# A hybrid decoder layer on one core: PSUM sets swapped from the first gate unit on, and one more seven-product pair per output unit

## Chip, cores and metric

One core of a Trainium2 chip. The metric is the device time of one execution in microseconds (us). TensorE (PE, matmuls; PEld is its weight load), VectorE (DVE), ScalarE (ACT), GpSimd (POOL) and SyncE (SP, which issues the weight transfers) each run their own queue of instructions in a fixed order and wait for each other by semaphores.

## The reference

The input x is 256 tokens by 4096 channels, all in f32.

```python
h = rmsnorm(x, ln_g)
proj = h @ w_in                      # 4096 x 12288
p_x, p_gate, q, k, v, a_gate, s_u, s_gate = split(proj)
y_pool = pool_mixer(p_x, w_pool, pool_scale)
y_attn = stick_breaking_attention(q, k, v)          # 16 heads of 128
y_ssm  = s5_mixer(s_u, ..., w_glu, b_glu)           # 1024 x 2048 GLU
y_pool = rmsnorm(y_pool, g_pool) * silu(p_gate)     # the same for the others
y = concatenate([y_pool, y_attn, y_ssm])
out = rmsnorm(x + y @ w_out, final_g)               # 4096 x 4096
```

Stick-breaking attention needs, for each head, the scores z, a softplus of them, a suffix sum of that over the keys, an exponential, and the product with v.

## The kernel before

**Matmuls.** Each f32 matmul is made of three in a faster format: a value is split into a rounded part hi and the rest lo, and hi·hi, hi·lo and lo·hi are added up in PSUM. For the weights ScalarE writes hi (L110, through `act`) and DVE subtracts to get lo (L98, through `tt`). The activations lie split in SBUF as xhl. A step streams a weight piece of 128 x 2 x 512 (512 KB, two k-tiles) by SP (`load`, L164), splits it (`split`), and multiplies it for both halves of the tokens (`mm_tok`, L273 to L275).

**Units.** The weights are passed through in units of 512 or 1024 columns: 16 narrow ones of w_in (512), the wide units w0 and w1 (1024: v, q and k of the last head groups), four GLU units of 8 k-tiles, the wide gate units w2 and w3, and four wide output units out0 to out3. A wide unit has 16 pairs s of k-tiles, each with two pieces (h = 0 and 1).

**Seven products.** In wide units the pairs in SEVEN use a Strassen-like scheme: a 2 x 2 block product of (two token halves) x (two k-tiles) x (two column halves) with 7 instead of 8 block products, 21 instead of 24 matmuls (`mm_seven`, L239). `split_seven` makes the differences t7 of the weights (four DVE operations of 512) and splits four combinations into ring entries. The activation sums y7 come from `row_sums`. Four of the products go to a second PSUM set and are added in at the end of the unit (`join_seven`).

**PSUM sets.** The wide part has four tiles of two banks each, b0 to b3. `start_bank` picks two for the sums of a unit; the other two are its side set, which takes the attention's scores and the transposes until the unit's first seven-product pair (s = 4), and the four products from there on. The GLU units sum in b2 and b3 in turn, and attention uses b0 and b1 meanwhile. A tile is free when the step that reads it has ended: for a GLU unit the addition of the bias on DVE (`gl`, in `finish`).

**Attention.** `attention` is a generator, advanced by `pump` beside the matmuls. Each head group has two pairs of heads. For one pair: scores and mask into ps_z on PE (L688 to L692), three steps on ScalarE (al), one on DVE (al, L107), a split (ah on ScalarE, ax on DVE), the suffix sum by PE into ps_z (L706 to L708), the exponential on ScalarE (aw), and ps_av on PE (L720 to L722). The last head group runs beside the GLU units.

**Placing.** The branch outputs come back as tiles yk and yT of 4 k-tiles and are split into xhl by `place(g)`, which also makes the row sums of the seven-product pairs. Six are taken back in w3; the last ones are put there by the gates in out0. At s = 7 of out0 `start_end` closes the pool `mid`; the loads of SP wait for its last readers.

**Rings.** Tag t4 in pool `base` has three places for t7, e7, and GLU tiles; tag k4 in `mid` has six for the tiles of the branches; the ring for split weights has 4 entries, 6 in wide units outside the GLU. The Tile scheduler sets the order of PE, DVE, ScalarE and POOL; only SP is written by hand.

Of the kernel before, what the change touches and what calls it, by code (L numbers as in the profile page):

```python
# [20 lines left out]
P = 128  # L21
# [13 lines left out]
RING_OUT = 6  # L35
K4 = 6
T4 = 3
SEVEN = (4, 6, 7, 9, 11, 13)
WIDE = 2 * NU
WIDE_KINDS = ("w0", "w1", "w2", "w3")  # L40
WARM = 8
# [27 lines left out]
def body(tc, a, out, ctx):  # L69
# [61 lines left out]

    xhl = xp.tile([P, KT, 2, L], F32R, name="xhl")

    def rsqrt_mean(dst, ss, n, mean_over, tp, tag):
        m = tp.tile([P, n], F32, tag=tag, bufs=3, name="rs_m")
        t = tp.tile([P, n], F32, tag=tag, bufs=3, name="rs_t")
        ts(m, ss, 1.0 / mean_over, ALU.mult, EPS, ALU.add)
        act(t, m, AF.Ln)
        act(dst, t, AF.Exp, scale=-0.5)
        tt(t, dst, m, ALU.mult)  # L140
        stt(t, t, -0.5, dst, ALU.mult, ALU.mult)
        stt(dst, t, 1.5, dst, ALU.add, ALU.mult)
# [41 lines left out]
        return s in sevens_of(*units[ui][:2])  # L184

    def sevens_of(kind, c):
        return SEVEN[1:] if (kind, c) == ("out", 0) else SEVEN if kind == "out" or kind in WIDE_KINDS else ()

    def flat(w):
        return w.rearrange("p k n -> p (k n)")  # L190
# [61 lines left out]

    def row_sums(s, xa, xb):
        where = state["rows"]
        t = where.tile([P, 3, P], F32, tag="t", bufs=1, name="ts")
        tt(t[:, 0, :], xa[:, P:L], xb[:, P:L], ALU.add)
        tt(t[:, 1, :], t[:, 0, :], xa[:, 0:P], ALU.subtract)
        tt(t[:, 2, :], xb[:, 0:P], t[:, 1, :], ALU.subtract)
        y = where.tile([P, 3, 2, P], F32R, tag="y%d" % s, bufs=1, name="y7")
        hi_lo(y[:, :, 0, :], y[:, :, 1, :], t)  # L260
        state["s7"][s] = y
# [618 lines left out]
        state["o"] = ep.tile([P, 2, D], F32, name="o")  # L880

    def start_bank(kind, c):
        first = {"w0": 2, "w1": 0, "w2": 0, "w3": 2}.get(kind, c % 2 * 2)
        state["side"] = 2 - first
        return [wide_bank(first + t, "pm") for t in range(2)]

# [15 lines left out]
    def finish(kind, c, n, ps):  # L902
# [5 lines left out]
        elif kind == "px":  # L908
            side_q.append(pool_unit(n, scaled(ps, "px")))
        elif kind == "pg":  # L910
            side_q.append(pool_gate(n, scaled(ps, "pgz")))
        elif kind == "sg":
            z = scaled(ps, "sgz")
            sgate[n] = dp.tile([P, 2, NU], F32, name="kept_s%d" % n)

            def sgate_gen(z=z, n=n):
                sg = mp.tile([P, 2, NU], F32, tag="k4", bufs=K4, name="sgm")
                sigmoid_of(z, sg)
                yield
                tt(z, z, sg, ALU.mult)  # L920
                G.dma_start(sgate[n], z)
                yield
            side_q.append(sgate_gen())
        elif kind == "v":
            cur["v"] = scaled(ps, "vt")
        elif kind in ("q", "k"):
            if n == 2:
                side_q.append(channels_away(kind, n, scaled(ps, kind + "z")))
                return
            t = mp.tile([P, 4, L], F32, tag="k4", bufs=K4, name=kind + "t")  # L930
            side_q.append(channels(scaled(ps, kind + "z"), t, QS if kind == "q" else 1.0))
            cur[kind] = t
            if kind == "k":
                if apool is None:
                    start_att()
                side_q.append(attention(n, cur["v"], cur["q"], cur["k"]))
        elif kind == "glu":
            bias = lp.tile([P, NU], F32, tag="bias", bufs=1, name="bias")
            side_dma(bias, a["bgl"][n:n + 1, :].partition_broadcast(P))
            y = bp.tile([P, 2, NU], F32, tag="t4", bufs=T4, name="gl")  # L940
            for t in range(2):
                tt(y[:, t, :], ps[t], bias, ALU.add)
            if n % 2 == 0:
                def gate_gen(y=y):
                    sg = bp.tile([P, 2, NU], F32, tag="t4", bufs=T4, name="gs")
                    glu["sg"] = sg
                    sigmoid_of(y, sg)
                    yield
                side_q.append(gate_gen())
            else:  # L950
                def val_gen(y=y, n=n):
                    tt(y, y, glu.pop("sg"), ALU.mult)
                    yield
                    square_sums(glu_sums, y, n // 2)
                    yield
                    glu[n // 2] = y
                    if n == 3:
                        r = branch_norm(glu_sums, 1024)
                        for u in range(2):
                            yu, sg = glu.pop(u), sgs[u]  # L960
                            for t in range(2):
                                stt(sg[:, t, :], yu[:, t, :], r[:, t:t + 1], sg[:, t, :], ALU.mult, ALU.mult)
                            gates.append(transposed(sg, keep(2 + u)))
                        yield
                sgs = []
                if n == 3:
                    for u in range(2):
                        sgs.append(mp.tile([P, 2, NU], F32, tag="k4", bufs=K4, name="sgb"))
                        G.dma_start(sgs[u], sgate[u])
                side_q.append(val_gen())  # L970
        elif kind in WIDE_KINDS:
            e = state["joined"]
            parts = [(k, scaled_wide(ps, e, h, k + "z")) for h, (k, _) in enumerate(WIDE_IN[c])]
            for h, (k, z) in enumerate(parts):
                if k == "v":
                    away("v", 2 + h, z.rearrange("p t (c m) -> p (t c) m", m=L))
                elif k in ("q", "k"):
                    t = mp.tile([P, 4, L], F32, tag="u4", bufs=2, name=k + "t")
                    side_q.insert(h, channels(z, t, QS if k == "q" else 1.0))
                    cur[k] = t  # L980
                else:
                    gates.append(att_gate(2 * (c - 2) + h, z))
            if c == 0:
                side_q.append(attention(2, *fetch(2, "vqk")))
            elif c == 1:
                side_q.append(attention(3, *fetch(3, "v"), cur["q"], cur["k"]))
        elif kind == "out":
            o, e, fg = state["o_n"], state["joined"], state["fg"]
            for t in range(2):
                tt(o[:, t, :], ps[t].rearrange("p h m -> p (h m)"), o[:, t, :], ALU.add)  # L990
                act(e[t].rearrange("p h m -> p (h m)"), o[:, t, :], AF.Square, accum_out=out_sums[:, t, n:n + 1])
            for t in range(2):
                tt(o[:, t, :], o[:, t, :], fg, ALU.mult)
# [21 lines left out]
    for i, (ui, s, h) in enumerate(subs):  # L1015
# [46 lines left out]
            split(split_to)  # L1062
            split_to += 1
        if ui == LATE_AT:
            if s in SEVEN:
                load_again(s)
            if s - 1 in SEVEN:
                sums_of_x(s - 1)
        if kind == "w3" and s in (2, 4, 6, 8, 10, 12) and h == 0:
            take_back(s // 2 - 1)  # L1070
# [1 line left out]
        if seven(i):  # L1072
            if h == 0:
                if s == sevens_of(kind, c)[0]:
                    assert not state["held"]
                    pp = products()
                mm_seven(i, s, ps, pp, s == sevens_of(kind, c)[0], s == SEVEN[-1])
                if s == SEVEN[-1]:
                    if kind == "out":
                        state["fg"] = load_fg(c)  # L1080
                    state["joined"] = join_seven(pp, state["o_n"] if kind == "out" else None)
        else:
            pair = htiles.pop(i)
            late = i >= N_SUB - HELD
            into = [ps[t][:, h, :] for t in range(2)] if wide else ps
            mm_tok(into, rows, (2 * s, 2 * s + 1), pair, s == 0, s == nk // 2 - 1, (0,) if late else (0, 1))
            if late:
                delayed.append((s, h, pair))
        if s == nk // 2 - 1 and h == (1 if wide else 0):
            n = nth.get(kind, 0)  # L1090
            nth[kind] = n + 1
# [26 lines left out]
                ssm_steps[0] += 1  # L1118

    o, last, fg = state["o"], state["o_n"], state["fg"]  # L1120
    sums = cp.tile([P, 2, 2], F32, name="last_sums")
    for t in range(2):
        for h in range(2):
            cols = slice(h * NU, h * NU + NU)
# [2 lines left out]
                    if h1 == h:  # L1127
                        mm_tok([None, ps[1][:, h, :]], xhl, (2 * s, 2 * s + 1), pair, False, s == KT // 2 - 1, (1,))
            tt(last[:, t, cols], ps[t][:, h, :], last[:, t, cols], ALU.add)
            act(state["joined"][t][:, h, :], last[:, t, cols], AF.Square, accum_out=sums[:, t, h:h + 1])  # L1130
        tt(out_sums[:, t, 3:4], sums[:, t, 0:1], sums[:, t, 1:2], ALU.add)
        r = cp.tile([P, 1], F32, name="r_out%d" % t)
        ss = cp.tile([P, 1], F32, name="ss_out%d" % t)
        V.tensor_reduce(ss, out_sums[:, t, :], mybir.AxisListType.X, ALU.add)  # L1134
        rsqrt_mean(r, ss, 1, D, cp, "rs")
        rows = slice(t * P, t * P + P)
        for at, wide, eng in ((0, 512, V), (512, 512, S), (1024, 1024, V), (2048, 1024, S), (3072, 1024, V)):
            cs = slice(at, at + wide)
# [110 lines left out]
```

## Time and profile before

| | |
|---|---|
| three runs, median (lowest to highest) | 1541.36 us (1539.26 to 1542.06) |
| the profiled execution | 1541.24 us |
| its span, first to last instruction | 1539.5 us |
| mean granted clock of TensorE | 0.993 |
| PE / DVE / ScalarE busy | 98% / 82% / 58% of the span |
| matmuls | 6827 |

The span is shorter than the execution by 1.7 us, which lie around it. In a row of a view, L273 is line 273 of the kernel; `pm<-hi,xhl` reads "written <- read", by the program's names without buffer numbers. A row of waits is: engine, what it was about to do, what ended the wait; total, times, longest. In a timeline row an idle time before the instruction stands in square brackets. Matmuls are pipelined, so the distance from start to start counts and not the length of a row.

### The profile page before, as it was taken

What the parts mean: (1) busy time and instruction counts of PE and PEld (TensorE: products, weight loads), DVE (VectorE), ACT (ScalarE), POOL (GpSimd) and SP (SyncE); (2) the same over time, 40 slices, a digit from 0 to 9 for tenths busy, and PEclk for the clock granted to TensorE, in tenths of its full rate; (3) what the DMA queues carried; (4) which work ended last, traced back from release to release, by engine and by line L of the source; (5) the groups of instructions that cost most, each with busy time, mean ns of one, the idle gap of its engine ahead of it and who ended that gap; (6) DMA issues with size and microseconds to landing.
All of it is one profiled execution on the core that took longest, in us unless ns stands there. A gap on an engine that the chain in (4) does not pass through costs nothing.

```text
span 1539.5 us, 19528 instructions
## 1 busy us (share of the span) xinstructions
PE 1513.6 (98%) x6827; PEld 1234.3 (80%) x6827; DVE 1267.7 (82%) x1933; ACT 897.4 (58%) x1194; POOL 20.4 (1%) x39
## 2 busy tenths in 40 slices
PE   9999999999999999999999999999999999999996
PEld 7888888888888887888787878778888878888885
DVE  7479878898988878987778787669899988988886
ACT  7655456665555655565655555756767654645453
POOL 0000000000000000000000000000000100000000
PEclk9999999999999999999999999999999999999998
DMA  9766656576666556655656756556586595666654
GB/s 356 298 227 198 203 173 209 182 223 214 207 199 197 185 166 207 199 178 160 235 192 204 266 172 223 169 213 244 170 296 219 187 332 169 234 196 207 211 198 171
DMA packets 99315, 326.70 MB, mean 212 GB/s; under 512 B 12368, under 2 KB 18256, under 8 KB 99216
## 3 DMA queue, kind: packets, MB, share of 16 engines
q1 hardware_dynamic: 84096, 296.44, 57.6%
q0 software_dynamic: 4976, 18.09, 3.1%
q10 hardware_dynamic: 10144, 10.92, 2.3%
q8 instruction: 53, 0.87, 0.2%
q14 instruction: 46, 0.38, 0.1%
HBM read 309.68 MB, written 12.58 MB: 209 GB/s over the span
## 4 chain that ended last, share of the span: by engine, by line
PE 90%; DVE 3%; DMA 3%; ACT 1%; issue 1%; SPq 0%; DVEq 0%; ACTq 0%
PE pm L273 24%; PE pm L274 24%; PE pm L275 24%; PE p L239 7%; PE pm L239 5%; DMA w<-in_ws 3%; DVE lo L98 2%; DVE t L98 1%; PE ps_y L649 1%; ACT hi L110 1%; PE ps_c L780 1%; PE ps_bu L622 0%; PE ps_z L688 0%; PE ps_p L431 0%; PE ps_t L340 0%
## 5 line engine op out<-in xcount | busy, mean ns | idle before, releaser
L110 ACT ACTIVATE hi<-w 128x1024 fp32r<-128x1024 f32 (+1 forms) x505 | 509.7, 1017 | 411.8 <-PE pm L275 335.3
L98 DVE TENSOR_TENSOR lo<-w,hi 128x1024 fp32r<-128x1024 f32 (+1 forms) x505 | 587.7, 1172 | 165.0 <-ACT hi L110 161.8
L274 PE MATMUL pm<-lo,xhl 128*128 128x512 f32 x1672 | 656.9, 393 | 0.7 <-DVE lo L98 0.7
L275 PE MATMUL pm<-hi,xhl 128*128 128x512 f32 x1672 | 655.7, 393 | 0.0
L273 PE MATMUL pm<-hi,xhl 128*128 128x512 f32 x1672 | 647.8, 393 | 1.3 <-DVE ss_out L1134 0.8
L273 PEld LDWEIGHTS pm<-hi,xhl 128*128 128x128 f32 x1672 | 315.1, 189 | 71.4 <-issue 2.9
L274 PEld LDWEIGHTS pm<-lo,xhl 128*128 128x128 f32 x1672 | 315.4, 189 | 69.3 <-issue 2.5
L275 PEld LDWEIGHTS pm<-hi,xhl 128*128 128x128 f32 x1672 | 315.2, 188 | 68.1 <-issue 2.1
L110 ACT ACTIVATE hi<-t 128x1024 fp32r<-128x1024 f32 x94 | 99.0, 1059 | 67.3 <-DVE t L98 26.2
L98 DVE TENSOR_TENSOR lo<-t,hi 128x1024 fp32r<-128x1024 f32 x94 | 113.4, 1222 | 12.8 <-ACT hi L110 12.2
L98 DVE TENSOR_TENSOR t<-w 128x512 f32<-128x512 f32 x84 | 54.4, 689 | 33.0 <-DMA w<-in_ws 32.9
L239 PE MATMUL p<-hi,y 128*128 128x512 f32 x188 | 74.1, 394 | 2.5 <-ACT hi L110 2.5
L239 PE MATMUL pm<-hi,xhl 128*128 128x512 f32 x188 | 74.1, 395 | 0.2 <-ACT hi L110 0.2
L239 PE MATMUL p<-hi,xhl 128*128 128x512 f32 x188 | 74.0, 395 | 0.0
L98 DVE TENSOR_TENSOR t<-w,t 128x512 f32<-128x512 f32 x84 | 57.7, 687 | 0.2
L107 DVE SCALAR_TENSOR_TENSOR et<-et,pw,tr 128x16 f32<-128x16 f32 (+3 forms) x256 | 55.5, 276 | 2.0 <-ACT tr L110 1.8
L110 ACT ACTIVATE tr<-et,pw 128x32 f32<-128x32 f32 (+3 forms) x128 | 44.1, 382 | 11.1 <-DVE et L107 6.8
L239 PEld LDWEIGHTS p<-hi,y 128*128 128x128 f32 x188 | 35.4, 188 | 11.6 <-ACT hi L110 3.8
L239 PEld LDWEIGHTS pm<-hi,xhl 128*128 128x128 f32 x188 | 35.3, 188 | 8.4 <-ACT hi L110 0.7
L239 PEld LDWEIGHTS p<-hi,xhl 128*128 128x128 f32 x188 | 35.5, 189 | 8.1
L637 DVE TENSOR_TENSOR_SCAN tb<-rho,ta 128x256 f32<-128x256 f32 x64 | 40.6, 677 | 0.3
L110 ACT ACTIVATE hi<-o 128x1024 fp32r<-128x1024 f32 (+1 forms) x26 | 25.0, 976 | 26.3 <-PE pm L275 21.5
(268 smaller groups left out, 1287.3 us busy)
## 6 DMA issues: line engine op xcount, KB each, us to landing
w<-in_ws SPq DMA_DIRECT2D x501, 512.0 KB, 4.2
o<-in_ws SPq DMA_DIRECT2D x26, 512.0 KB, 4.3
xsq<-in_xr SPq DMA_DIRECT2D x8, 512.0 KB, 6.7
o<-in_xr POOLq DMA_DIRECT2D x8, 512.0 KB, 11.1
xt<-in_xT SPq DMA_DIRECT2D x15, 256.0 KB, 6.1
b<-in_bst ACTq DMA_DIRECT2D x16, 192.0 KB, 4.4
u<-uT ACTq DMA_DIRECT2D x96, 32.0 KB, 2.7
kept<-yT POOLq DMA_DIRECT2D x6, 512.0 KB, 6.0
```

Source lines behind the costliest of these rows:

```text
L98: V.tensor_tensor(o, x, y, op)
L107: V.scalar_tensor_tensor(o, x, s, y, op0, op1)
L110: return S.activation(o, x, f, **kw)
L239: T.matmul(o, stat[:, p, :], pair[q][:, n], start=start and k == 0, stop=stop and k == 2, skip_group_check=True)
L273: T.matmul(ps[t], stat[:, slot, 0, sl], hi[:, n], start=begin, stop=False, skip_group_check=True)
L274: T.matmul(ps[t], stat[:, slot, 0, sl], lo[:, n], start=False, stop=False, skip_group_check=True)
L275: T.matmul(ps[t], stat[:, slot, 1, sl], hi[:, n], start=False, stop=end, skip_group_check=True)
L637: V.tensor_tensor_scan(tb[:, c, :], rho[:, pr:pr + 1].broadcast_to([P, L]), ta[:, c, :], 0.0, ALU.mult, ALU.add)
L649: T.matmul(ps[32 * j:32 * j + 32, 0:L], cf[:, j, c, :], ss[j][:, c, :], start=c == 0, stop=c == 1, skip_group_check=True)
L780: T.transpose(ps[:, (c * 2 + t) * P:(c * 2 + t + 1) * P], z[:, t, (h * 2 + c) * P:(h * 2 + c + 1) * P], ident)
```

## The change

1. SEVEN, which the output units use, becomes (4, 6, 7, 9, 10, 12, 13): seven pairs in out1 to out3, six in out0 (without s = 4). The units w0 to w3 use SEVEN_IN = (4, 6, 7, 9, 10, 13): six as before, with 10 in the place of 11.
2. From w2 on the PSUM sets are swapped: w2 sums in b2 and b3, w3 in b0 and b1, the output units alternate from b2 and b3. As b3 is held by the last GLU unit, the first pair of w2 is staggered: token half 0 of both pieces first, token half 1 after.
3. The ts tile of `row_sums` moves from the pool `rows` into the ring t4, the GLU bias tile from the pool `late` into the ring k4.
4. At the end the sum of squares of the first column half goes into out_sums, whose reduction is done early; that of the second half is added inside the normalisation.

```diff
-SEVEN = (4, 6, 7, 9, 11, 13)
+SEVEN = (4, 6, 7, 9, 10, 12, 13)
+SEVEN_IN = (4, 6, 7, 9, 10, 13)
...
-    def rsqrt_mean(dst, ss, n, mean_over, tp, tag):
+    def rsqrt_mean(dst, ss, n, mean_over, tp, tag, plus=EPS):
...
-        ts(m, ss, 1.0 / mean_over, ALU.mult, EPS, ALU.add)
+        ts(m, ss, 1.0 / mean_over, ALU.mult, plus, ALU.add)
...
-        return SEVEN[1:] if (kind, c) == ("out", 0) else SEVEN if kind == "out" or kind in WIDE_KINDS else ()
+        if kind == "out":
+            return SEVEN if c else SEVEN[1:]
+        return SEVEN_IN if kind in WIDE_KINDS else ()
...
-        t = where.tile([P, 3, P], F32, tag="t", bufs=1, name="ts")
+        t = bp.tile([P, 3, P], F32, tag="t4", bufs=T4, name="ts")
...
-        first = {"w0": 2, "w1": 0, "w2": 0, "w3": 2}.get(kind, c % 2 * 2)
+        first = {"w0": 2, "w1": 0, "w2": 2, "w3": 0}.get(kind, 2 - c % 2 * 2)
...
-            bias = lp.tile([P, NU], F32, tag="bias", bufs=1, name="bias")
+            bias = mp.tile([P, NU], F32, tag="k4", bufs=K4, name="bias")
...
+            border = kind == "w2" and at < 2
             into = [ps[t][:, h, :] for t in range(2)] if wide else ps
-            mm_tok(into, rows, (2 * s, 2 * s + 1), pair, s == 0, s == nk // 2 - 1, (0,) if late else (0, 1))
-            if late:
+            mm_tok(into, rows, (2 * s, 2 * s + 1), pair, s == 0, s == nk // 2 - 1, (0,) if late or border else (0, 1))
+            if late or border:
                 delayed.append((s, h, pair))
+            if border and at == 1:
+                for s1, h1, pair in delayed:
+                    mm_tok([None, ps[1][:, h1, :]], rows, (2 * s1, 2 * s1 + 1), pair, s1 == 0, False, (1,))
+                delayed.clear()
...
-    sums = cp.tile([P, 2, 2], F32, name="last_sums")
+    sums = cp.tile([P, 2, 1], F32, name="last_sums")
...
-            act(state["joined"][t][:, h, :], last[:, t, cols], AF.Square, accum_out=sums[:, t, h:h + 1])
-        tt(out_sums[:, t, 3:4], sums[:, t, 0:1], sums[:, t, 1:2], ALU.add)
+            act(state["joined"][t][:, h, :], last[:, t, cols], AF.Square, accum_out=(sums if h else out_sums)[:, t, 3 * (1 - h):4 - 3 * h])
+            if h == 0:
+                ss = cp.tile([P, 1], F32, name="ss_out%d" % t)
+                V.tensor_reduce(ss, out_sums[:, t, :], mybir.AxisListType.X, ALU.add)
+                ts(ss, ss, 1.0 / D, ALU.mult, EPS, ALU.add)
...
-        ss = cp.tile([P, 1], F32, name="ss_out%d" % t)
-        V.tensor_reduce(ss, out_sums[:, t, :], mybir.AxisListType.X, ALU.add)
-        rsqrt_mean(r, ss, 1, D, cp, "rs")
+        rsqrt_mean(r, sums[:, t, 0:1], 1, D, cp, "rs", plus=ss)
```

In `load_again` and `sums_of_x` SEVEN becomes SEVEN_IN too.

The scheduler puts the instructions of the changed kernel in another order. On PE at the last GLU unit, before: pm_8874 are the sums of glu3, ps_z_8652 and ps_av_8694 the first attention pair, ps_z_8720 the second (the rows from the end of glu3 on).

```order
L275 MATMUL pm_8874<-hi_8895,hhl_8488 128x512
L706 MATMUL ps_z_8652<-ah_8664,tneg_81 128x512
L707 MATMUL ps_z_8652<-ah_8664,oneneg_82 128x2x128
...
L720 MATMUL ps_av_8694<-vt_8482,aw_8692 128x128
...
L688 MATMUL ps_z_8720<-qt_8480,kt_8481 128x256
...
L692 MATMUL ps_z_8720<-maskb_84,identb_83 128x256
L706 MATMUL ps_z_8720<-ah_8755,tneg_81 128x512
```

After, pm_8767 being glu2 (its last matmuls come first here, and the rows go on to the start of glu3):

```order
L277 MATMUL pm_8767<-lo_8802,hhl_8488 128x512
L278 MATMUL pm_8767<-hi_8801,hhl_8488 128x512
L709 MATMUL ps_z_8652<-ah_8664,tneg_81 128x512
L710 MATMUL ps_z_8652<-ah_8664,oneneg_82 128x2x128
...
L723 MATMUL ps_av_8694<-vt_8482,aw_8692 128x128
...
L691 MATMUL ps_z_8720<-qt_8480,kt_8481 128x256
...
L695 MATMUL ps_z_8720<-maskb_84,identb_83 128x256
L276 MATMUL pm_8874<-hi_8829,hhl_8488 128x512
L277 MATMUL pm_8874<-lo_8830,hhl_8488 128x512
```

The first pair's suffix sum and ps_av, which stood behind glu3, now stand ahead of it; the second pair's step from ah_8755 moved from directly behind its mask to behind 43 matmuls of glu3.

On ScalarE at the same place, before (al, ah and aw of the first pair, then al of the second; bias_8947 is the bias of glu3):

```order
L110 ACTIVATE al_8659<-ps_z_8652 128x768
L110 ACTIVATE hi_8895<-w_8845 128x1024
L110 ACTIVATE al_8659<-al_8659 128x768
L110 ACTIVATE gs_8868<-gl_8865 128x1024
L75 DMA bias_8947<-in_bgl 128x512
...
L110 ACTIVATE ah_8664<-al_8659 128x768
...
L110 ACTIVATE aw_8692<-ps_z_8652 128x768
L110 ACTIVATE al_8727<-ps_z_8720 128x768
```

After, with the biases of glu1, glu2 and glu3 (bias_8749, bias_8863, bias_8947):

```order
L111 ACTIVATE al_8659<-ps_z_8652 128x768
L111 ACTIVATE hi_8895<-w_8845 128x1024
L111 ACTIVATE al_8659<-al_8659 128x768 x2
L111 ACTIVATE ah_8664<-al_8659 128x768
L111 ACTIVATE aw_8692<-ps_z_8652 128x768
L76 DMA bias_8749<-in_bgl 128x512
L76 DMA bias_8863<-in_bgl 128x512
L76 DMA bias_8947<-in_bgl 128x512
L111 ACTIVATE al_8727<-ps_z_8720 128x768
```

The issues of three biases now stand in a row behind aw_8692, the exponential of the first pair.

On DVE in w3, before, behind lo_10091 and the first row sum (w_10047 and w_10074 are the two plain pieces of pair 10; lo_10190 to lo_10194 and t7_10185 belong to the seven-product pair 11; ts_10106 is a row sum):

```order
L98 TENSOR_TENSOR lo_10153<-w_10047,hi_10152 128x1024
L98 TENSOR_TENSOR t7_10185<-w_10136,w_10080 128x512
L98 TENSOR_TENSOR t7_10185<-w_10136 128x512
L98 TENSOR_TENSOR ts_10106<-ts_10106,yk_10104 128x128
L98 TENSOR_TENSOR yk_10104<-yk_10104 128x128
L98 TENSOR_TENSOR lo_10093<-t7_10083,hi_10092 128x1024
L98 TENSOR_TENSOR t7_10186<-w_10136,t7_10185 128x512
L98 TENSOR_TENSOR lo_10180<-w_10074,hi_10179 128x1024
L98 TENSOR_TENSOR ts_10106<-yk_10104,ts_10106 128x128
L98 TENSOR_TENSOR lo_10190<-w_10080,hi_10189 128x1024
L98 TENSOR_TENSOR lo_10192<-w_10136,hi_10191 128x512
L98 TENSOR_TENSOR lo_10194<-t7_10185,hi_10193 128x1024
```

After (lo_10161 and lo_10163 are the t7 combinations of pair 10, which is a seven-product pair now; ts_10106 and ts_10114 are the row sums of the two pairs placed there, yk_10104 the tile they come from, lo_10245 and lo_10263 pieces of later pairs):

```order
L99 TENSOR_TENSOR t7_10152<-w_10074,w_10047 128x512
L99 TENSOR_TENSOR t7_10152<-w_10074 128x512
L99 TENSOR_TENSOR ts_10114<-yk_10104,ts_10114 128x128
L99 TENSOR_TENSOR xhl_102<-yk_10104,xhl_102 128x4x256
L99 TENSOR_TENSOR y7_10110<-ts_10106,y7_10110 128x3x128
L99 TENSOR_TENSOR lo_10245<-w_10150,hi_10244 128x1024
L99 TENSOR_TENSOR lo_10161<-t7_10152,hi_10160 128x1024
L99 TENSOR_TENSOR t7_10153<-w_10074,t7_10152 128x512
L99 TENSOR_TENSOR y7_10118<-ts_10114,y7_10118 128x3x128
L99 TENSOR_TENSOR lo_10263<-w_10195,hi_10262 128x1024
L99 TENSOR_TENSOR t7_10153<-w_10047,t7_10153 128x512
L99 TENSOR_TENSOR lo_10163<-t7_10153,hi_10162 128x1024
```

The row sums of two pairs and the split of the placed tile (xhl_102) now lie between the first piece of pair 10 and its combinations lo_10161 and lo_10163.

More of the change, by code (lines that the diff above doesn't have):

```diff
@@ L1064, in body @@
         if ui == LATE_AT:
-            if s in SEVEN:
+            if s in SEVEN_IN:
                 load_again(s)
-            if s - 1 in SEVEN:
+            if s - 1 in SEVEN_IN:
                 sums_of_x(s - 1)
```

## The prediction

> **What bounds the kernel now.** The page comes first: span, busy times, the chain that ended last, one group of the matmuls.
>
> ```profile
> span 1539.5 us, 19528 instructions
> PE 1513.6 (98%) x6827; PEld 1234.3 (80%) x6827; DVE 1267.7 (82%) x1933; ACT 897.4 (58%) x1194; POOL 20.4 (1%) x39
> PE 90%; DVE 3%; DMA 3%; ACT 1%; issue 1%; SPq 0%; DVEq 0%; ACTq 0%
> ```
>
> TensorE sets the time. So a change pays by fewer matmuls or by shorter idle time of PE, and costs what it adds to that idle time. PE's waits are few; these three are the largest in the middle of the kernel:
>
> ```profile
> PE ps_z L706 <- ACT ah L110: 4.6, 1, 4.6
> PE p L239 <- ACT hi L110: 2.5, 2, 2.0
> PE ps_av L720 <- ACT aw L110: 1.9, 2, 1.0
> ```
>
> The first and the third lie at the border from the last GLU unit (glu3) to w2, the second in the first output unit (out0). The windows view shows what a wait drags behind it, and how full VectorE is. Columns: stretch, length, PE, PEld, DVE, ACT, POOL busy, granted clock, DMA share, GB/s.
>
> ```profile
> 993.50:1010.97 17.47, 10.79 (x52) 9.07 (x51) 9.89 (x13) 8.60 (x12) 0.38 (x1) 0.80 0.48 181
> 1239.00:1243.00 4.00, 4.00 (x12) 3.13 (x11) 3.49 (x5) 1.72 (x3) 0.00 (x0) 0.57 1.02 396
> 853.00:940.00 87.00, 86.33 (x384) 69.96 (x383) 69.86 (x79) 47.78 (x53) 2.66 (x5) 1.00 0.65 221
> 1094.00:1180.00 86.00, 86.00 (x382) 70.02 (x381) 81.10 (x101) 61.35 (x74) 1.08 (x2) 1.00 0.66 226
> 1180.00:1266.00 86.00, 83.97 (x365) 67.83 (x364) 75.14 (x95) 55.50 (x68) 5.85 (x9) 0.98 0.71 251
> 1142.50:1161.00 18.50, 18.50 (x81) 14.98 (x81) 18.50 (x27) 12.07 (x13) 0.00 (x0) 1.00 0.85 281
> ```
>
> Rows three to five are w1, w3 and out0. The last row is the middle of w3: PE and DVE are both busy for all of its 18.5 us. DVE has nothing to spare there; whatever is put ahead of a piece that PE needs next is paid by PE.
>
> **Fewer matmuls: -2.8 us.** A plain pair is 24 matmuls, a seven-product pair 21. Out0 goes from five such pairs to six and out1 to out3 from six to seven: 4 x 3 = 12 matmuls fewer. Their spacing is read from PE's timeline in w3, first and last of 41 steps:
>
> ```profile
> 1144.18 0.40 PE L274 MATMUL pm<-lo,xhl 128*128 128x512 f32 x1
> 1153.71 0.39 PE L239 MATMUL p<-hi,xhl 128*128 128x512 f32 x1
> ```
>
> (1153.71 - 1144.18) / 41 = 0.2324 us, times 12 is 2.8 us. (The 0.39 in the row is the length of one; they overlap.)
>
> **The tail: -0.4 us.** Between the last ScalarE sum and the normalisation stand two small DVE operations:
>
> ```profile
> 1529.10 0.16 DVE L98 TENSOR_TENSOR out_sums<-last_sums 128x1 f32<-128x1 f32 x1 [0.79 <-ACT e L110]
> 1529.30 0.16 DVE L1134 TENSOR_REDUCE ss_out<-out_sums 128x1 f32<-128x4 f32 x1
> 1529.49 0.15 DVE L104 TENSOR_SCALAR rs_m<-ss_out 128x1 f32<-128x1 f32 x1
> ```
>
> The reduction now uses the half that is ready earlier, and the addition is gone: 1529.49 - 1529.10 = 0.4 us.
>
> **The border: a stall that moves.** Rows of PE, then of ScalarE, around it:
>
> ```profile
> 981.50 0.27 PE L692 MATMUL ps_z<-maskb,identb 128*128 128x256 bf16 x1
> 993.53 0.39 PE L706 MATMUL ps_z<-ah,tneg 128*128 128x512 f32 x1
> 995.59 0.49 PE L720 MATMUL ps_av<-vt,aw 128*128 128x128 f32 x2 [0.96 <-ACT aw L110]
> 997.03 0.60 PE L688 MATMUL ps_z<-qt,kt 128*128 128x256 f32 x2
> 998.45 0.27 PE L692 MATMUL ps_z<-maskb,identb 128*128 128x256 bf16 x1
> 1003.30 0.51 PE L706 MATMUL ps_z<-ah,tneg 128*128 128x512 f32 x1 [4.58 <-ACT ah L110]
> 1010.81 0.40 PE L274 MATMUL pm<-lo,xhl 128*128 128x512 f32 x1
> ```
>
> ```profile
> 982.39 0.79 ACT L110 ACTIVATE al<-ps_z 128x768 f32<-128x768 f32 x1
> 983.08 1.05 ACT L110 ACTIVATE hi<-w 128x1024 fp32r<-128x1024 f32 x1
> 998.82 0.81 ACT L110 ACTIVATE al<-ps_z 128x768 f32<-128x768 f32 x1 [3.28 <-PE ps_z L692]
> 1005.55 0.81 ACT L110 ACTIVATE aw<-ps_z 128x768 f32<-128x768 f32 x1 [2.31 <-PE ps_z L708]
> 1006.25 1.99 ACT L110 ACTIVATE hi<-w 128x1024 fp32r<-128x1024 f32 x2
> ```
>
> Now: the attention of the last head group has two pairs. Glu3's matmuls lie between the first pair's mask (981.50) and its next step (993.53) and hide that chain. The second pair's chain is bare. From 993.53 to 1010.81 pass 17.3 us; ah and ax of two pairs (2 x 0.94), two ps_av (2 x 1.4), one ps_z (1.5) and four w2 matmuls (0.9) are about 7.1 us of them. 10.2 us are lost.
>
> After: swapping the sets and staggering w2's first pair should put work under the second chain, and by the order it does (43 matmuls of glu3 stand ahead of its ah, token 0 of w2 behind). But the bias tiles now come from the ring of six, whose free places wait for the attention output's store, and three bias issues stand on ScalarE behind the first pair's aw. Queued behind them there are the second pair's al and the weight copies. The DVE step that adds a bias frees bank 3, and glu3 writes bank 3. So PE takes the whole first pair with only five matmuls of glu2 as cover. Its path: the second pair's bare chain took 1003.30 - 998.45 = 4.85 us from mask to ah; the first pair adds 0.5 (982.39 - 981.50 instead of 998.82 - 998.45) and one weight copy, 0.95. Ah reaches PE at 981.5 + 6.3 = 987.8. From there to aw 2.25 (1005.55 - 1003.30), aw itself 0.7: bias issue at 990.75. What a bias needs:
>
> ```profile
> L98 DVE TENSOR_TENSOR gl<-pm,bias x8: 680/682/692, 955.4 to 994.3; 128x512 f32<-128x512 f32 x8
> DMA to landing us min/median/max: 3.5/4.2/5.4
> ```
>
> Landing at 994.3 to 996.2, two additions 1.3, and glu3 starts at 995.6 to 997.5, middle 996.3. Without waits it would start after the mask (0.1), five matmuls (1.2) and 3.9 of attention work, at 986.7. Lost: 8.9 to 10.8, middle 9.6, against 10.2 before; up to 1.6 more if the clock is still halved when glu3 starts. Net -1.3 to +2.2; I take 0. The Trainium skill ("SBUF — State Buffer", "The DMA setup-cost knee") gives about 2 us plus bytes over 436 GB/s for a transfer, 2.6 us for these 256 KB, an estimate from that page; by it the border would gain 1.6 more, but the trace's four landings, 3.5 to 5.4 us, are slower and decide.
>
> **W3: +4.8 us.** SEVEN_IN has 10 where 11 stood, so pairs 9 and 10 are neighbours. A seven costs DVE four 512-wide differences, one 512 and three 1024-wide subtractions, a plain pair two of 1024. Pitches, start to start:
>
> ```profile
> 1143.67 1.23 DVE L98 TENSOR_TENSOR lo<-t,hi 128x1024 fp32r<-128x1024 f32 x1
> 1144.81 0.69 DVE L98 TENSOR_TENSOR t<-w,t 128x512 f32<-128x512 f32 x1
> 1145.41 0.29 DVE L98 TENSOR_TENSOR ts<-yk 128x128 f32<-128x128 f32 x1
> 1145.61 1.23 DVE L98 TENSOR_TENSOR lo<-w,hi 128x1024 fp32r<-128x1024 f32 x1
> 1154.90 0.56 DVE L98 TENSOR_TENSOR y<-ts,y 128x384 fp32r<-128x384 f32 x1
> 1155.37 1.23 DVE L98 TENSOR_TENSOR lo<-w,hi 128x1024 fp32r<-128x1024 f32 x1
> ```
>
> 1.14, 0.60, 0.20 and 0.47 for 1024, 512, 128 and 384: a seven is 5 x 0.60 + 3 x 1.14 = 6.42 us on DVE and 21 x 0.2324 = 4.88 on PE; a plain pair 2.28 and 5.58. Two sevens in a row use up 3.1 us of DVE's lead. Up to the row at 1143.67 (lo_10091) both programs run the same order. From there the new order puts six 1024, four 512, eight 128 and one 384 up to lo_10161 (6.84 + 2.40 + 1.60 + 0.47 = 11.3): done at 1155.0. The ts tiles sit in the ring of three that the t7 pieces use, so t7_10152 and t7_10153 come late, behind two row sums. PE reaches lo_10161 37 matmuls after 1144.18, at 1152.8: it waits 2.2. The same count gives 1158.9 against 1154.4 for lo_10163 (4.6), 1160.3 against 1155.6 for lo_10200 (4.7, or 4.8 with the part by which an operation outlasts its pitch). The waits overlap; in all 4.8. Below 3.2 only if DVE brings a lead of more than 2 us to 1143.67, and above 4.8 only with a slowed clock behind it, 6.4.
>
> **Out0: -0.4 us.** Before:
>
> ```profile
> SPq L164 <- DVE xhl L98: 17.1, 3, 11.8
> 1225.86 10.40 DMA w<-in_ws
> 1238.42 0.49 PE L239 MATMUL p<-hi,y 128*128 128x512 f32 x1 [2.01 <-ACT hi L110]
> ```
>
> The SP queue stood 11.8 us until the mid tiles were free, then the loads came in a burst (a transfer of 10.4 us), a ScalarE copy waited, PE idled 2.0 us and ran 3.4 us at the 0.57 clock window above, where a matmul takes 0.43: another 3.4 x (1 - 0.23 / 0.43) = 1.6. These 3.6 us should go, since the placing steps now end a pair earlier. In their stead a sixth seven: in pairs 6 to 13 DVE needs 6 x 6.42 + 2 x 2.28 = 43.1 us against PE's 40.4; with five it was 38.9 against 41.1. The swing is 4.9, the upper end; the lower is 0. Counting the rows with the pitches leaves DVE 1.5 to 1.9 behind; with a slowed clock 3.2. Net -3.6 to +1.3; I take -0.4.
>
> **The rest: +0.3.** Neighbouring sevens in w0 to w2 and out1 to out3 find DVE less full (69.86 of 87 us in w1): 0 to 1.
>
> Sum: -2.8 - 0.4 + 0 + 4.8 - 0.4 + 0.3 = +1.5 against the profiled execution's 1541.24 us (span 1539.5 and 1.7 around it; 0.1 below the median of the runs): 1542.7, or 1542.9 beside the median. Of this kernel 0.2% (3.1 us) is about what can be told from no change.
>
> **The rivals.** *Faster: DVE keeps its lead.* If the order in w3 costs PE nothing, 4.8 go: 1538.1; if bias transfers also land before the attention ends, 3.4 more: 1534.7. For it: the scheduler had this order to choose, and out0 loses its burst. Against it: the row of 18.5 full DVE microseconds. It decides where DVE leads by 5.3 us at lo_10077 rather than by the 0.5 counted. Chance 0.24.
>
> *Slower: each new wait halves the clock.* After the 2.0 us wait PE ran 3.4 us at half pace. W3's waits (2.2, then 2.4) and glu3's late start would each do the same: +1.6, +1.6, and out0 at its upper end +1.7: 1547.8. It decides from waits of about 2 us. Chance 0.30. The Trainium skill ("TensorE: Matmul & The Clock Gate", "What's actually happening") says the clock halves after an idle window of about 3.4 us; by that w3's waits would be too short and this rival loses 1.6. The trace has a half clock after a wait of 2.0, so I let the row decide.
>
> *The stagger does nothing*, since the stall only moves to the glu2 border: that is part of the forecast. Had it fallen away whole, 10.2 less: 1532.7; the order of PE, with ah ahead of glu3, speaks against that.
>
> **How the numbers follow.** Forecast 1542.9 with a chance of 0.46 and a range of its own of 1538.5 to 1545. 0.24 lie on the faster side and 0.30 on the slower. Within 0.2% is 1538.3 to 1544.4, which holds most of the forecast's range: same 0.42, faster 0.24, slower 0.34. The range 1534 to 1548.5 leaves out a tenth on each side.
>
> **What would show it.** Right: PE waits on ah (about 4.9 us) ahead of glu3 and on a bias addition right before it, none ahead of w2; waits on lo at 1152 to 1160 in w3 that add up to 4.8; no 11.8 us of SP in out0, with some waits on lo instead. Wrong: no PE wait in w3 on DVE, or glu3 starting by 987.

## The result

The changed kernel takes 1553.31 us in the median (1552.09 to 1554.55), the kernel before beside it 1541.32 us (1539.26 to 1542.06). The ratio is 1.008, with a 95% interval of 1.0062 to 1.0097: 12 us slower, where +1.5 us were forecast and 1548.5 us was the upper end.

The page of the profiled execution (1554.55 us):

```profile
span 1552.8 us, 19543 instructions
PE 1515.8 (98%) x6815; PEld 1231.4 (79%) x6815; DVE 1283.3 (83%) x1962; ACT 902.3 (58%) x1203; POOL 20.5 (1%) x39
PE 89%; DVE 5%; ACT 3%; DMA 2%; issue 1%; DVEq 0%; ACTq 0%; SPq 0%
```

There are 12 matmuls fewer, as intended, and yet the span is 13.3 us longer; in the chain that ended last the share of DVE went from 3% to 5% and that of ScalarE from 1% to 3%. PE's largest waits, after:

```profile
PE p L242 <- ACT hi L111: 5.1, 7, 2.7
PE ps_z L709 <- ACT ah L111: 4.7, 1, 4.7
PE pm L277 <- DVE lo L99: 3.7, 4, 2.5
PE p L242 <- DVE lo L99: 2.0, 2, 1.4
PE ps_c L783 <- ACT kz L111: 1.7, 2, 1.1
PE pm L276 <- DVE gl L99: 1.2, 1, 1.2
```

The wait on ah is still there. New are the waits on lo, 5.7 us in sum, where the whole kernel before had 0.7, and the waits on hi have doubled from 2.5 us.

**Where the time went.** The table sums, stage by stage, by how much each start-to-start distance on PE exceeds the usual one (0.232 us for 512 columns, 0.118 for 256, 0.110 for 128; excesses under 0.03 left out). It so holds idle time and halved clock together. A wait ahead of the first matmul of a unit is counted with that unit. The last line is the time from PE's end to the end of the span.

| us lost | before | after | |
|---|---|---|---|
| end of the last narrow unit, and w0 | 3.0 | 9.7 | +6.7 |
| w1 | 2.0 | 3.4 | +1.4 |
| glu2 and glu3 | 10.3 | 10.4 | +0.1 |
| w2 | 1.1 | 3.4 | +2.2 |
| w3 | 0.5 | 8.0 | +7.6 |
| out0 | 4.4 | 1.8 | -2.5 |
| out3 | 1.1 | 0.0 | -1.1 |
| behind PE's end | 12.7 | 15.3 | +2.6 |

With -0.5 in the first 15 units and 12 x 0.232 = 2.8 for the matmuls this is +13.7 against +13.3 in the spans.

**The glu2 border**, PE and ScalarE after:

```profile
988.79 0.27 PE L695 MATMUL ps_z<-maskb,identb 128*128 128x256 bf16 x1
994.95 0.80 PE L709 MATMUL ps_z<-ah,tneg 128*128 128x512 f32 x1 [4.72 <-ACT ah L111]
998.06 0.79 PE L723 MATMUL ps_av<-vt,aw 128*128 128x128 f32 x2 [0.90 <-ACT aw L111]
1003.16 0.48 PE L276 MATMUL pm<-hi,hhl 128*128 128x512 f32 x1
```

```profile
997.20 0.81 ACT L111 ACTIVATE aw<-ps_z 128x768 f32<-128x768 f32 x1 [2.31 <-PE ps_z L711]
997.26 1.32 ACTq L76 DMA_DIRECT2D bias<-in_bgl  x3
```

```profile
1001.63 1.28 DVE L99 TENSOR_TENSOR gl<-pm,bias 128x512 f32<-128x512 f32 x2
```

As forecast, the stall has moved: 6.2 us from mask to ah (6.3 forecast), three bias issues at aw, glu3 14.4 us behind the mask (14.8). One sign that the prediction named is missing: PE does not wait on the bias addition ahead of glu3. The addition ended at 1002.9, and PE, which did its attention work at half clock (the granted clock was 0.62 from 989.83 to 1003.40), was done with that at 1003.1. The two paths ended 0.2 us apart. The wait on gl in the list above (1.2 us) comes 20 us later, in w2.

**W0.** PE's waits there, and SP's (the loads of weights, and by L297 those of xs, the x tiles for the row sums):

```profile
781.60 0.50 PE L277 MATMUL pm<-lo,xhl 128*128 128x512 f32 x1 [0.54 <-DVE lo L99]
787.11 0.50 PE L277 MATMUL pm<-lo,xhl 128*128 128x512 f32 x1 [2.50 <-DVE lo L99]
```

```profile
SPq L297 <- DVE ts L99: 14.5, 1, 14.5
SPq L297 <- DVE y L99: 4.1, 1, 4.1
```

The ring t4 has more users than the section on the rings lists: xs is one of them. An xs load stood 14.5 us because a ts tile held its place, and every weight load behind it on SP stood too. Before, xs waited as well, 12.2 us at the same place, but on its own predecessors:

```profile
SPq L294 <- DVE xhl L98: 16.2, 3, 12.2
```

So the length of the wait is not the loss. What changed is when SP went on, first before, then after:

```profile
752.50 0.33 SPq L294 DMA_DIRECT2D xs<-in_xT  x1
```

```profile
754.53 0.33 SPq L297 DMA_DIRECT2D xs<-in_xT  x1
```

It went on 2.0 us later, and 2.4 us later with the last xs (759.13 and 761.52). In w0 a late weight then reaches PE: DVE waits for it, and the lo that it makes after that is the one that ends PE's 2.5 us at 787.11:

```profile
784.03 1.29 DVE L99 TENSOR_TENSOR t<-w 128x512 f32<-128x512 f32 x2 [2.49 <-DMA w<-in_ws]
785.84 1.22 DVE L99 TENSOR_TENSOR lo<-w,hi 128x1024 fp32r<-128x1024 f32 x1
```

How 2.0 to 2.4 us on SP became 6.7 us on PE was not followed step by step. The half clock behind the waits is a part of it: ten matmuls from 787.11 to 791.11 took 4.0 us where 2.3 is usual.

**W3**, waits of PE in order and a window behind them:

```profile
1162.76 0.50 PE L242 MATMUL p<-hi,y 128*128 128x512 f32 x1 [0.53 <-ACT hi L111]
1164.89 0.50 PE L242 MATMUL p<-lo,y 128*128 128x512 f32 x1 [1.40 <-DVE lo L99]
1168.78 0.80 PE L242 MATMUL p<-hi,y 128*128 128x512 f32 x1 [2.70 <-ACT hi L111]
```

```profile
1165.00:1173.00 8.00, 5.30 (x14) 3.73 (x15) 6.69 (x10) 4.86 (x5) 0.00 (x0) 0.59 0.80 290
787.70:790.80 3.10, 3.10 (x9) 2.40 (x8) 2.83 (x3) 0.00 (x0) 0.00 (x0) 0.50 0.75 200
```

The first row is w3, the second w0 behind its 2.5 us wait. In w0 the granted clock was a half. In w3 it was 0.59 over 8.0 us; if it was either whole or a half there, it was a half for 8.0 x 0.41 / 0.5 = 6.6 us.

What the last and longest of the three waits in w3 waited for, on DVE and then on ScalarE:

```profile
1166.96 0.68 DVE L99 TENSOR_TENSOR t<-w,t 128x512 f32<-128x512 f32 x1
1167.67 1.06 ACT L111 ACTIVATE hi<-t 128x1024 fp32r<-128x1024 f32 x1 [3.61 <-DVE t L99]
```

From 1148.8 to 1167.6 DVE had no gap. It was late with t7, and ScalarE stood 3.6 us for it.

**The tail.** Additions of the joined products and of the sums to the output on DVE, first before, then after:

```profile
1518.50 1.23 DVE L98 TENSOR_TENSOR o<-o,e 128x1024 f32<-128x1024 f32 x1
1520.66 1.29 DVE L98 TENSOR_TENSOR o<-pm,o 128x512 f32<-128x512 f32 x2 [0.94 <-PE pm L275]
```

```profile
1532.37 1.23 DVE L99 TENSOR_TENSOR o<-o,e 128x1024 f32<-128x1024 f32 x1
1533.69 0.69 DVE L99 TENSOR_TENSOR o<-pm,o 128x512 f32<-128x512 f32 x1
1534.81 1.29 DVE L99 TENSOR_TENSOR o<-pm,o 128x512 f32<-128x512 f32 x2 [0.42 <-PE pm L278]
```

Before, the join ended 7.0 us ahead of the end of PE's last matmul (1526.77), and token half 0 could be normalised and sent while PE made half 1. After, with a seventh pair and 12 and 13 as neighbours at the end of out3, it ends 3.9 us ahead of PE's end (1537.49); half 0 is late, and half 1 waits on DVE behind it.

### The profile page after: what moved, and what is told of

Read it like the earlier page. It is cut to its first block, busy times and chain, and to the rows that moved or that the text cites. A ratio compares the mean times of both kernels' runs of the same rounds, so it can differ in the third digit from the quotient of the medians.

```text
span 1552.8 us, 19543 instructions
## 1 busy us (share of the span) xinstructions
PE 1515.8 (98%) x6815; PEld 1231.4 (79%) x6815; DVE 1283.3 (83%) x1962; ACT 902.3 (58%) x1203; POOL 20.5 (1%) x39
## 4 chain that ended last, share of the span: by engine, by line
PE 89%; DVE 5%; ACT 3%; DMA 2%; issue 1%; DVEq 0%; ACTq 0%; SPq 0%
PE pm L276 24%; PE pm L277 24%; PE pm L278 24%; PE p L242 7%; PE pm L242 6%; DVE lo L99 2%; DMA w<-in_ws 1%; ACT hi L111 1%; DVE t L99 1%; PE ps_y L652 1%; PE ps_c L783 1%; PE ps_bu L625 0%; PE ps_p L434 0%; PE ps_z L691 0%; PE ps_t L343 0%
## 5 line engine op out<-in xcount | busy, mean ns | idle before, releaser
L277 PE MATMUL pm<-lo,xhl 128*128 128x512 f32 x1640 | 643.9, 393 | 3.7 <-DVE lo L99 3.7
L278 PE MATMUL pm<-hi,xhl 128*128 128x512 f32 x1640 | 642.3, 392 | 0.0
L276 PE MATMUL pm<-hi,xhl 128*128 128x512 f32 x1640 | 635.2, 393 | 2.1 <-DVE gl L99 1.2
L277 PEld LDWEIGHTS pm<-lo,xhl 128*128 128x128 f32 x1640 | 308.9, 188 | 72.8 <-DVE lo L99 6.1
L276 PEld LDWEIGHTS pm<-hi,xhl 128*128 128x128 f32 x1640 | 308.9, 188 | 71.7 <-issue 2.9
L278 PEld LDWEIGHTS pm<-hi,xhl 128*128 128x128 f32 x1640 | 308.9, 188 | 66.5 <-issue 2.1
L111 ACT ACTIVATE hi<-t 128x1024 fp32r<-128x1024 f32 x102 | 106.9, 1058 | 103.6 <-DVE t L99 60.3
L99 DVE TENSOR_TENSOR lo<-t,hi 128x1024 fp32r<-128x1024 f32 x102 | 122.7, 1218 | 13.4 <-ACT hi L111 13.2
L242 PE MATMUL p<-hi,y 128*128 128x512 f32 x204 | 81.4, 399 | 4.9 <-ACT hi L111 4.9
L99 DVE TENSOR_TENSOR t<-w 128x512 f32<-128x512 f32 x90 | 58.0, 685 | 31.2 <-DMA w<-in_ws 31.1
L242 PE MATMUL pm<-hi,xhl 128*128 128x512 f32 x204 | 80.7, 397 | 0.3 <-ACT hi L111 0.2
L242 PE MATMUL p<-hi,xhl 128*128 128x512 f32 x204 | 79.4, 394 | 0.2 <-ACT hi L111 0.2
L242 PEld LDWEIGHTS pm<-hi,xhl 128*128 128x128 f32 x204 | 38.6, 189 | 9.5 <-ACT hi L111 1.2
L242 PE MATMUL p<-lo,y 128*128 128x512 f32 x102 | 40.8, 400 | 2.0 <-DVE lo L99 2.0
```

The costliest lines, as they stand in the source:

```text
L99: V.tensor_tensor(o, x, y, op)
L111: return S.activation(o, x, f, **kw)
L242: T.matmul(o, stat[:, p, :], pair[q][:, n], start=start and k == 0, stop=stop and k == 2, skip_group_check=True)
L276: T.matmul(ps[t], stat[:, slot, 0, sl], hi[:, n], start=begin, stop=False, skip_group_check=True)
L277: T.matmul(ps[t], stat[:, slot, 0, sl], lo[:, n], start=False, stop=False, skip_group_check=True)
L278: T.matmul(ps[t], stat[:, slot, 1, sl], hi[:, n], start=False, stop=end, skip_group_check=True)
```

## The experiments

Two theories at the start. A: the tiles that moved into shared rings (ts, bias) cost the time, the swap by itself is good. B: the denser seven-product pairs cost it. Medians of each run, with the kernel before timed on the same chip:

| run | us | before | ratio (95%) |
|---|---|---|---|
| swap_only | 1536.43 | 1541.17 | 0.9966 (0.9951 to 0.9981) |
| swap_bias | 1537.94 | 1541.17 | 0.9973 (0.9963 to 0.9983) |
| ts_only | 1546.30 | 1541.17 | 1.0029 (1.0018 to 1.0040) |
| old_sevens | 1543.41 | 1541.17 | 1.0011 (1.0001 to 1.0021) |
| ts_back | 1546.51 | 1540.87 | 1.0038 (1.0026 to 1.0051) |
| neighbours_12_13 | 1545.26 | 1540.87 | 1.0027 (1.0018 to 1.0035) |
| no_swap | 1555.09 | 1540.87 | 1.0091 (1.0077 to 1.0104) |
| swap_tail | 1535.65 | 1540.87 | 0.9963 (0.9950 to 0.9977) |
| xs_elsewhere | 1545.66 | 1541.80 | 1.0026 (1.0017 to 1.0035) |
| ts_split | 1534.02 | 1541.80 | 0.9953 (0.9939 to 0.9967) |

The time lost on PE by stage, worked out as above ("border" is glu2, glu3 and w2; w0 includes the end of the unit ahead of it):

| us lost | w0 | w1 | border | w3 | out0 | behind PE |
|---|---|---|---|---|---|---|
| before | 3.0 | 2.0 | 11.4 | 0.5 | 4.4 | 12.7 |
| after | 9.7 | 3.4 | 13.7 | 8.0 | 1.8 | 15.3 |
| swap_only | 2.8 | 2.0 | 8.4 | 0.5 | 4.5 | 12.7 |
| swap_bias | 2.7 | 2.0 | 12.5 | 0.5 | 0.5 | 12.7 |
| ts_only | 9.8 | 2.0 | 13.3 | 0.8 | 1.9 | 12.7 |
| old_sevens | 8.5 | 2.0 | 12.7 | 0.8 | 2.1 | 11.5 |
| ts_back | 3.1 | 3.4 | 12.3 | 2.4 | 8.9 | 15.4 |
| neighbours_12_13 | 6.4 | 2.0 | 12.1 | 1.7 | 4.0 | 15.3 |
| no_swap | 8.3 | 3.2 | 17.2 | 8.4 | 2.2 | 15.3 |
| swap_tail | 2.9 | 2.0 | 8.8 | 0.5 | 3.1 | 11.5 |
| xs_elsewhere | 2.1 | 3.2 | 12.6 | 8.8 | 1.9 | 15.2 |
| ts_split | 2.1 | 2.0 | 7.5 | 0.8 | 2.0 | 11.4 |

**swap_only.** The kernel before with the swap and the stagger. These lines switch them on; the other lines of the stagger are those of the change:

```diff
-        first = {"w0": 2, "w1": 0, "w2": 0, "w3": 2}.get(kind, c % 2 * 2)
+        first = {"w0": 2, "w1": 0, "w2": 2, "w3": 0}.get(kind, 2 - c % 2 * 2)
...
+            border = kind == "w2" and at < 2
```

> The kernel before with the swapped PSUM sets and w2's staggered first pair alone; the seven-product pairs, the ts tile, the bias tile and the tail stay as they were. Theory A (what cost time are the two tiles that moved into shared rings; the swap by itself is good): the order of PE puts glu3 under the first attention pair and w2 under the second, no wait on ah above 1 us, 8 to 10 us fewer at the border, 1531 to 1534 us. Theory B (the loss comes from the denser seven-product pairs, the swap has no worth): 1540 to 1543 us.

4.7 us faster, between the ranges of A and B. The wait on ah is gone from glu2 and glu3, as A has it, but not all of the 8 to 10 us came: the border as a whole gained 3.0, since w2 now loses 8.0 us, 6.8 more than before. Rows of its PE:

```profile
1026.17 0.41 PE L343 MATMUL ps_t<-ident,sgb 128*128 128x128 f32 x2 [1.69 <-issue]
1028.26 1.39 PE L343 MATMUL ps_t<-ident,sgb 128*128 128x128 f32 x8 [0.60 <-ACT yT L111]
```

The gate tiles (sgb) are transposed there, and waits on lo follow. That these steps used to be hidden in the long stall and now meet w2's matmuls is a reading that no run tested.

**swap_bias.** The same, and the bias tile in the ring:

```diff
-            bias = lp.tile([P, NU], F32, tag="bias", bufs=1, name="bias")
+            bias = mp.tile([P, NU], F32, tag="k4", bufs=K4, name="bias")
```

> The same as the run before it, and the bias tile of the GLU units in the ring k4. Theory A: the bias issues move behind the first pair's exponential, PE waits 4.5 to 5 us on ah ahead of glu3 and the gain is gone, 1540 to 1543 us, 8 to 10 above the run without it. Theory B: the bias tile is harmless, within 1.5 us of the run without it.

The stall is back at glu2 (a wait of 4.7 us on ah), the border loses 12.5 instead of 8.4. The total rose by only 1.5 us, which the intervals of the two runs do not tell from nothing, since out0 lost 0.5 instead of 4.5 in this order. So A is right on the mechanism and wrong on the total, which is where B had it.

**ts_only.** The kernel before with the ts tile in t4:

```diff
-        t = where.tile([P, 3, P], F32, tag="t", bufs=1, name="ts")
+        t = bp.tile([P, 3, P], F32, tag="t4", bufs=T4, name="ts")
```

> The kernel before with the ts tile of the row sums in the ring t4, nothing else. Theory A: the loads of xs for the row sums at the end of the last narrow unit wait for places in that ring, SP stands longer and w0 waits on lo as in the changed kernel: 4 to 7 us more, 1545 to 1548 us, nearly all of it between 755 and 800 us. Theory B: at w0 the neighbouring pairs 9 and 10 did it, and this changes nothing there, 1540 to 1543 us.

5.1 us slower; w0 loses 9.8, as in the changed kernel, with the old pairs. At w0 B has fallen.

**old_sevens.** The changed kernel with the old pairs:

```diff
-SEVEN = (4, 6, 7, 9, 10, 12, 13)
-SEVEN_IN = (4, 6, 7, 9, 10, 13)
+SEVEN = (4, 6, 7, 9, 11, 13)
+SEVEN_IN = (4, 6, 7, 9, 11, 13)
```

> The changed kernel with the old pairs (4, 6, 7, 9, 11, 13) in all wide units, so 12 more matmuls (2.8 us). Theory A: the losses of the two rings stay (6 at w0, 0.6 at the border against the kernel before), those of w3 and of the tail go: 1546 to 1550 us. Theory B: nearly all losses go, 1539 to 1543 us.

9.9 us come back, despite 12 more matmuls, and the total lies just above B's range, well below A's. W0 stays near what A says (8.5); w3 falls to 0.8, and the tail to 11.5 us, under the 12.7 of before. So each theory holds for a part: the pairs cost 7 us in w3, 3.8 in the tail and 1.4 in w1 (back at 2.0 here), the ring 5 to 7 at w0. Which of the new pairs, or their number, makes the tail late was not tried apart. From here on: C, these have nothing to do with each other; D, in w3 it takes both.

**ts_back.** The changed kernel with ts in its old place, and, for room, a constant's raw tile in k4:

```diff
-        t = bp.tile([P, 3, P], F32, tag="t4", bufs=T4, name="ts")
+        t = where.tile([P, 3, P], F32, tag="t", bufs=1, name="ts")
...
-            raw = cp.tile([P, P], F32, name="raw", tag="rb", bufs=1)
+            raw = mp.tile([P, P], F32, tag="k4", bufs=K4, name="raw")
```

> The changed kernel with the ts tile back in the pool of the row sums (a constant tile of the start lies in the ring k4 instead, to make room). Theory C (two losses that have nothing to do with each other: the ring costs 6.7 us at w0, the neighbouring pairs 9 and 10 cost 8.0 in w3): the loss before and in w0 falls from 9.7 to about 3, w3 stays at 8: 1546 to 1548 us. Theory D (the shared ring makes the neighbours dear, since the t7 pieces of pair 10 wait for places that ts tiles hold): by the order and the pitches the wait at pair 10 falls from 4.7 to 1.7, the loss in w3 to 2 to 4: 1540 to 1543 us.

W0 falls to 3.1 and w3 to 2.4, as D has it; PE's largest wait at pair 10:

```profile
PE p L242 <- DVE lo L99: 0.8, 1, 0.8
```

So in w3 it takes both: 0.5 with neither, 0.8 with the ring alone (ts_only), 2.4 with the pairs alone, 8.0 with both. The total is above D's range, in C's by chance, because out0 now loses 8.9 us. There SP stands longer than before:

```profile
SPq L165 <- DVE xhl L99: 14.6, 1, 14.6
```

In the changed kernel, with ts in the ring, SP's longest wait there is 8.4 us and out0 loses 1.8. In ts_only out0 loses less too (1.9 instead of 4.4). So the ring that harms w0 goes with a cheaper out0 in both comparisons. It is not the only way there: in swap_bias out0 loses 0.5 with ts in its old place.

**neighbours_12_13.** The changed kernel, w0 to w3 with other pairs:

```diff
-SEVEN_IN = (4, 6, 7, 9, 10, 13)
+SEVEN_IN = (4, 6, 7, 9, 12, 13)
```

> The changed kernel with (4, 6, 7, 9, 12, 13) in w0 to w3: pair 12 in the place of 10, so that the neighbours come where three pairs without them stand before. Theory C: pairs 12 and 13 have a fuller lead of DVE, the loss in w3 falls to 3 or less, that at w0 stays: 1547 to 1549 us. Theory D: ts tiles are made near pair 12 of w3 too, the loss only moves: 1550 to 1554 us.

Faster than either theory said. W3 loses 1.7, so neighbours and ring together are not enough; the place of the neighbours counts. That it is the row sums of two placed pairs which make pair 10 the dear place fits the order of DVE, but no run moved the row sums by themselves. W0 fell to 6.4, which neither theory gave.

**no_swap.** The changed kernel with the old sets and no stagger:

```diff
-        first = {"w0": 2, "w1": 0, "w2": 2, "w3": 0}.get(kind, 2 - c % 2 * 2)
+        first = {"w0": 2, "w1": 0, "w2": 0, "w3": 2}.get(kind, c % 2 * 2)
...
-            border = kind == "w2" and at < 2
+            border = False
```

> The changed kernel with the old PSUM sets and no stagger. The order shows the stall on ah ahead of glu3 in this one too, since the bias tile is still in the ring k4. If the bias tile takes the whole worth of the swap, within 2 us of the changed kernel, 1552 to 1555 us; if the swap still brings something behind that stall, 3 to 5 more, 1556 to 1559 us.

1.8 us above the changed kernel, with intervals that overlap: the total does not tell the two readings apart. By the profile the swap still brings 3.5 us at the border (13.7 instead of 17.2), about what it brought in swap_only (3.0). So there the two add up: the swap saves 3.0 to 3.5 us, and the bias tile costs about 4 (12.5 in swap_bias against 8.4).

**swap_tail.** swap_only and the new tail:

```diff
+            act(state["joined"][t][:, h, :], last[:, t, cols], AF.Square, accum_out=(sums if h else out_sums)[:, t, 3 * (1 - h):4 - 3 * h])
...
+        rsqrt_mean(r, sums[:, t, 0:1], 1, D, cp, "rs", plus=ss)
```

> The kernel before with the swap, the stagger and the new tail; the ts tile, the bias tile and the seven-product pairs as before. If the new tail is worth what the run with the old pairs showed behind its last matmul (11.5 us instead of 12.7), 1.2 less than the swap alone: 1535 us, and the fastest of all so far. If the tail is hidden by the output transfers, 1536.5 us.

Behind PE's end 11.5 instead of 12.7, so the new tail is worth 1.2 us by the profile where the join is early. The median fell by 0.8 between runs on two chips, too little to tell from nothing.

**xs_elsewhere.** The changed kernel with the xs tiles out of t4:

```diff
-        xs = bp.tile([P, 2, L], F32, tag="t4", bufs=T4, name="xs")
+        xs = mp.tile([P, 2, L], F32, tag="k4", bufs=K4, name="xs")
```

> The changed kernel, its ts tiles still in the ring t4, but the xs tiles that are loaded again for the row sums in the ring k4. If the loss at w0 comes from xs loads and ts tiles sharing three places (SP stands on a ts tile with the weight loads behind it), it falls from 9.7 to 3 to 4 us and the kernel to 1546 to 1548 us. If ts in the ring delays DVE by itself, the loss stays: 1552 to 1555 us. W3 stays at about 8 either way.

As the first reading has it, with a total just under its range: w0 loses 2.1, ts still in the ring. PE's only wait over 0.5 us left from 715 to 860 us, and w3 unchanged at 8.8:

```profile
PE ps_c L783 <- ACT kz L111: 0.6, 1, 0.6
```

So at w0 it is not ts in the ring by itself, but ts and xs in the same three places. SP's longest wait at this place falls from 14.5 to 4.0 us.

**ts_split.** swap_tail, and ts in the ring only where tiles are placed:

```diff
-                row_sums(s, t[:, 2 * h, :], t[:, 2 * h + 1, :])
+                row_sums(s, t[:, 2 * h, :], t[:, 2 * h + 1, :], bp.tile([P, 3, P], F32, tag="t4", bufs=T4, name="ts"))
```

> The swap, the stagger and the new tail with the old seven-product pairs and the old bias tile, and the ts tile in the ring t4 only where tiles are placed (w3 and out0), while the row sums at w0 keep their own tile. The runs so far say that the ring helps out0 (1.8 to 2.1 us lost instead of 3.1 to 4.5, with SP not standing on the last tiles) and harms w0 alone: w0 at 3, w3 below 1, out0 near 2, 1533 to 1535 us, 1 to 2.5 below the swap with the new tail. If out0's gain came from the ring's effect at w0, 1535.5 to 1537.

1534.02 us, ratio 0.9953: 7.8 us faster than the kernel before, and the lowest median of all, though its interval overlaps those of swap_tail and swap_only. W0 2.1, w3 0.8, out0 2.0, as expected or better.

## Why the prediction was wrong

- **Matmuls, -2.8.** Right: 12 fewer.
- **The border, 0.** Right in place and size: glu2 and glu3 lose 10.4 against 10.3. The stall moved and the bias tile moved it (swap_only against swap_bias). Of the path behind it, bias, addition, glu3, the last step did not bind: PE's own work at half clock ended 0.2 us later. That the size came out so well is therefore partly luck. Not forecast were 2.2 us in w2. There, PE's waits on hi and lo (0.5 and 0.55 us) stand in swap_bias as well, which has the old ts tile and the old pairs, so they go with the swap and the bias tile. The third, 1.2 us on glu3's bias addition (gl), is in none of swap_bias, old_sevens, ts_back and xs_elsewhere; its cause stays open.
- **W3, +4.8.** The place and the mechanism were right: t7 pieces behind ts tiles, at pair 10 (ts_back, old_sevens), and DVE without a gap. The three waits sum to 4.6 us, nearly the 4.8 forecast. The term was still mis-sized, 7.6, for what follows the waits: the clock did halve (0.59 over 8 us), which the sum left out and the upper end took as 1.6.
- **Out0, -0.4.** PE's old wait of 2.0 us went, as said, and the sixth pair cost less than was taken: -2.5. The reason given, placing steps that end a pair earlier, is not what the runs show: ts_back has the same pairs and loses 8.9, with SP standing 14.6 us. SP still stands 8.4 us in the changed kernel.
- **The tail, -0.4.** Wrong in sign. "The reduction now uses the half that is ready earlier, and the addition is gone" is true, and by the profile worth 1.2 (swap_tail). But the new pairs of out3, with 12 and 13 at its end, were not followed to the end: they make DVE's join late, which costs 3.8 (old_sevens), and +2.6 comes out.
- **"The rest: +0.3".** This is the step that failed. Neighbouring pairs were weighed for w0 to w2, 0 to 1 us for all of them, and for w1 alone that was nearly right (+1.4, from the pairs: 2.0 with the old ones). But the ts tile was followed only into w3, and at w0 its move was put at nothing. Its ring is also that of xs, whose loads SP issues between the weights, and SP's queue was not walked there. It cost +6.7 us (ts_only +6.8 with the old pairs; with xs out of the ring w0 loses 2.1).

The rival "each new wait halves the clock" gave the right side and part of the cause: it happened in w3 and ahead of glu3, as it said, and in w0, which it did not name, but not in out0 (granted clock 1.00 from 1200 to 1286). Its 1547.8 is still 5.5 us short. The Trainium skill ("TensorE: Matmul & The Clock Gate", "What's actually happening") has the clock halve after an idle window of about 3.4 us; here it halved after waits of 2.5 us (w0) and of 1.4 and 2.7 with work between (w3), so the measurement decides against a need for 3.4 us without work.

Left open: why w0 lost 6.4 and not 9.7 with neighbours_12_13, though xs stood 14.4 us on a ts tile there too, and what a part of out0's differences between 0.5 and 8.9 us is due to beyond SP's long wait; each run has another order there.

## What to carry to other kernels

When a tile moves into a shared ring, list all who allocate from that ring, and for each one that is filled by a load walk the queue that issues it: what stands behind the waiting load goes out late, and what that costs depends on how far ahead it was. A gain in one place can be undone by the space it needs elsewhere; try each part alone before the sum. And look at the last unit by itself: there work saved on the busiest engine can be lost by making the other one finish later.

## What the runs showed of the hardware

The granted clock of TensorE was 0.50 in the 3.1 us behind a wait of only 2.5 us. A bias load of 256 KB landed in 3.2 to 4.1 us in the changed kernel (3.5 to 5.4 before):

```profile
DMA to landing us min/median/max: 3.2/3.5/4.1
```
